# The down projection of a gated MLP as seven block products with sums formed in place, in place of twenty-two chunk steps

## The chip, the cores and the metric

The kernel runs on one core of one Trainium2 chip. The metric is the device time of one execution in microseconds (us); the time of a kernel is the median of its runs. Five engines work side by side: TensorE (PE) multiplies matrices, VectorE (DVE) and ScalarE (ACT) work on elements, GpSimd (POOL) is hardly used here, and SyncE (SP) issues the transfers. Each engine takes its instructions in one fixed order, and a wait at one instruction holds up all that stand behind it on that engine. All transfers of the part that is looked at here are issued on SP.

## The reference

The reference is one layer of a decoder trunk on 1024 tokens of width 1024 (`D`): four mixers, a gated merge, an output projection and a gated MLP. Only the end of the MLP is touched:

```python
D_FF = 256 * ((8 * D_MODEL // 3 + 255) // 256)      # 2816
# h = h + RMSNorm(GatedMLP(RMSNorm(h))), with a causal depthwise conv before the activation
def _rmsnorm(x, g):
    xf = x.astype(F32)
    y = xf * lax.rsqrt(jnp.mean(xf * xf, axis=-1, keepdims=True) + RMS_EPS)
    return (y * g.astype(F32)).astype(x.dtype)
```

The down projection multiplies the activated features, 1024 x 2816, by `f_down`, 2816 x 1024. Its result is normalised over the 1024 outputs of a token, scaled by a vector, and added to the residual h.

## The kernel before

**Three passes.** Every large float32 product is made of three passes in the format fp32r. A tile is split by `B.split`: ACT copies it into a high part (helper line L230), and DVE subtracts that from the tile to get the low part (L1190). `B.mm` then issues high by high, high by low and low by high into one PSUM bank (all matmuls are recorded at helper line L233). A tile that both engines have split is called cut below.

**Order.** The instructions of each engine are put in order when the kernel is built, by the scheduler of the tile framework, which simulates a timeline; pools and their buffer counts decide which tiles wait for which.

**The up projection** runs over 22 chunks of 128 features (`NFF`). It is already computed with seven block products in place of eight. For each chunk and each half of the tokens DVE and ACT make conv, activation and product, and the result `cg` (128 features x 512 tokens, last operation at L1645) is stored to the DRAM buffer `ad` (L1646). Feature chunk f of the activations is `ad[f]`, 128 x 1024 tokens.

**The down projection before** (L1670 to L1740) takes the outputs in two halves of 4 tiles of 128. *Half 0* runs over the 22 chunks: it loads 128 x 512 of `f_down` (tile `d`, L1682) and 128 x 1024 of `ad` (tile `w`, L1199), cuts both, and issues 24 matmuls of 512 columns for 4 output tiles and 2 token halves; all 8 PSUM banks collect sums over the 22 chunks. *Half 1* does the other 4 output tiles in three token blocks of 512, 256 and 256; the cut weights `drh`, `drl` are kept from the first block. After a block, `drain` copies the banks out (ACT), squares them (ACT) and adds the squares (DVE, L1703); `finish` sums the squares over the outputs with matmuls by ones, takes the inverse root (ACT Ln and Exp, each behind a load of its table, and four short DVE operations, L277 to L280, on the tile `nt`), spreads it with transposes (`ident`, L239), multiplies (L1708), adds the residual `hr` (L1709) and stores (L1710). `finish` of a block is placed inside the next block's matmuls.

Of the kernel before, what the change touches and what calls it, by code (L numbers as in the profile page):

```python
# [1225 lines left out]
def build(tc, I, out):  # L1226
# [443 lines left out]
    dp = ctx.enter_context(k.pool("dw", 2, side="right"))  # L1670
    hp = ctx.enter_context(k.pool("hres"))
    acp = ctx.enter_context(k.pool("acc"))
    wr = ctx.enter_context(k.pool("dres", side="right"))
    acc = [acp.tile([128, SEQ], F32, name=f"acc{n}") for n in range(KD)]
    HF = SEQ // 2
# [1 line left out]
    wres = {}

    def down_w(f, half):
        B.n += 1  # L1680
        r = dp.tile([128, 512], F32, tag="d0", name=f"d0_{half}{f}", bufs=3)
        nc.sync.dma_start(r[:], I["f_down"][128 * f:128 * f + 128, 512 * half:512 * half + 512])  # L1682
        if half:
            h, l = (wr.tile([128, 512], F32R, name=f"dr{q}{f}") for q in "hl")
        else:
            h, l = (dp.tile([128, 512], F32R, tag=f"d{q}", name=f"d{q}{f}") for q in "hl")
        B.split(r[:], h[:], l[:])
        return wtiles((h, l), 4)

    def drain(n, a, b, p, i):  # L1690

        L = b - a
        k.act(acc[n][:, a:b], p, AF.Copy)
        for c in ([(a, b)] if a < HF else [(HF, HF + TB), (HF + TB, SEQ)] if L > TB else [(a, b)]):
            key = (c, n % 2)
            m = c[1] - c[0]
            if n < 2:
                ss[key] = hp.tile([128, m], F32, name=f"fs{c[0]}_{n}")
                k.act(ss[key][:], acc[n][:, c[0]:c[1]], AF.Square)
            else:  # L1700
                sq = hp.tile([128, HF], F32, tag="fq", name=f"fq{c[0]}_{n}", bufs=2)
                k.act(sq[:, :m], acc[n][:, c[0]:c[1]], AF.Square)
                TT(ss[key][:], ss[key][:], sq[:, :m], ALU.add)  # L1703

    def finish(a, b, h):
        rs = rms_of(k, [ss[(a, b), 0][:], ss[(a, b), 1][:]], b - a)
        for n in range(KD):
            STT(acc[n][:, a:b], acc[n][:, a:b], k.V("n3", n), rs, ALU.mult, ALU.mult)  # L1708
            TT(h[:, n], h[:, n], acc[n][:, a:b], ALU.add)  # L1709
            nc.sync.dma_start(out[128 * n:128 * n + 128, a:b], h[:, n])  # L1710
# [47 lines left out]
```

## Time and profile before

| | us |
|---|---|
| median of 3 runs (1912.21 to 1915.57) | 1914.32 |
| the profiled execution, its own time | 1908.61 |
| its span from the first instruction to the last | 1906.8 |
| mean granted clock of TensorE in it, share of full speed | 0.983 |
| last matmul of the up projection starts | 1638.95 |
| last matmul of the down projection ends | 1890.9 |

The durations below are those of the profiled execution, whose own time lies 5.7 us under the median; 1.8 us of it lie outside the span. The down projection is the last stage: from the end of the up projection's matmuls to the end of its own it takes 251.7 us, and what follows (the last block's normalisation and stores) 15.9 us.

### The profile page before, as it was taken

How to read it: one execution, taken by the hardware profiler on the slowest of the kernel's cores; microseconds unless marked ns; L12 is line 12 of the kernel's file. 1: busy time of each engine (PE TensorE's matmuls, PEld its weight loads, DVE VectorE, ACT ScalarE, POOL GpSimd, SP SyncE). 2: the span in 40 equal slices, each digit the busy share in tenths (PEclk: the TensorE clock that was granted, in tenths of full speed). 3: DMA queues.
4: the chain of work that ended last, by engine and by line, in shares of the span. 5: the costliest groups of instructions: out<-in, count | busy, mean ns of one | idle time of the engine just before them, and what ended most of it. 6: DMA issues, size and time to landing. Idle time of an engine off the chain costs nothing.

```text
span 1906.8 us, 33092 instructions
## 1 busy us (share of the span) xinstructions
PE 1825.1 (96%) x13476; PEld 1714.7 (90%) x13476; DVE 1240.8 (65%) x2454; ACT 783.9 (41%) x1176; POOL 58.4 (3%) x87
## 2 busy tenths in 40 slices
PE   8999999999999998999999997799999999999997
PEld 7899999888888898989999897699999999888896
DVE  6566477562464557686368558899899998534444
ACT  4532121121361326363246476545444544324433
POOL 0000000000000000000025000000000000000000
PEclk9999999999999998999999899899999999999998
DMA  5024574574542143232676412223222222545433
GB/s 178 35 80 145 167 240 146 164 210 129 182 150 92 61 135 113 79 112 68 210 231 201 146 43 69 83 67 95 75 93 87 80 90 81 191 139 181 151 126 106
DMA packets 138761, 239.69 MB, mean 126 GB/s; under 512 B 22280, under 2 KB 82224, under 8 KB 137968
## 3 DMA queue, kind: packets, MB, share of 16 engines
q1 hardware_dynamic: 138608, 237.57, 39.1%
q8 instruction: 106, 1.74, 0.4%
q14 instruction: 47, 0.39, 0.1%
HBM read 166.02 MB, written 71.51 MB: 125 GB/s over the span
## 4 chain that ended last, share of the span: by engine, by line
PE 81%; DVE 7%; ACT 5%; DMA 3%; issue 2%; POOL 1%; SPq 0%; DVEq 0%; ACTq 0%; POOLq 0%
PE pm L233 47%; PE px L233 20%; PE py L233 13%; ACT L230 2%; ACT h_e L230 1%; POOL mg L1416 1%; PE px L239 1%; DMA s_ub<-s_su 0%; PE py L239 0%; DMA sb_h<-gd 0%; DVE acc L1708 0%; DVE ml L1190 0%; DMA h_rq<-p_h 0%; DMA p_h<-stg_h 0%; DMA p_m<-stg_m 0%
## 5 line engine op out<-in xcount | busy, mean ns | idle before, releaser
L233 PE MATMUL pm<-uh,w 128*128 128x342 f32 (+2 forms) x2688 | 660.6, 326 | 23.2 <-ACT w L230 8.3
L233 PEld LDWEIGHTS pm<-uh,w 128*128 128x128 f32 x2688 | 470.9, 190 | 33.5 <-ACT w L230 8.5
L233 PE MATMUL pm<-ul,w 128*128 128x342 f32 (+2 forms) x1344 | 439.9, 327 | 1.4 <-DVE ul L1260 1.4
L233 PEld LDWEIGHTS pm<-ul,w 128*128 128x128 f32 x1344 | 255.4, 190 | 8.6 <-issue 2.6
L230 ACT ACTIVATE w<-w 128x1024 fp32r<-128x1024 f32 (+2 forms) x111 | 116.3, 1048 | 290.1 <-PE pm L233 210.6
L1190 DVE TENSOR_TENSOR w<-w,w 128x1024 fp32r<-128x1024 f32 (+2 forms) x111 | 134.7, 1214 | 78.7 <-ACT w L230 77.4
L230 ACT ACT_TABLE_LOAD x78 | 100.1, 1283 | 8.0 <-DMA r_cb<-r_db 2.5
L233 PE MATMUL pm<-mh,woh 128*128 128x256 f32 (+1 forms) x192 | 55.5, 289 | 2.0 <-ACT woh L230 1.8
L233 PE MATMUL px<-w,drh 128*128 128x256 f32 (+1 forms) x220 | 57.2, 326 | 0.0
L233 PE MATMUL pm<-ml,woh 128*128 128x256 f32 (+1 forms) x192 | 55.5, 289 | 0.0
L233 PE MATMUL pm<-mh,wol 128*128 128x256 f32 (+1 forms) x192 | 54.8, 286 | 0.0
L1190 DVE TENSOR_TENSOR dl<-d,dh 128x512 fp32r<-128x512 f32 x22 | 15.2, 693 | 59.1 <-ACT dh L230 59.1
L233 PE MATMUL px<-w,dh 128*128 128x512 f32 x132 | 51.4, 396 | 0.0
L233 PE MATMUL pm<-w,dh 128*128 128x512 f32 x132 | 51.3, 396 | 0.0
L230 ACT ACTIVATE cg<-zg,fvec 128x512 f32<-128x512 f32 x44 | 35.6, 809 | 20.1 <-DVE zg L1638 20.0
L233 PE MATMUL pm<-w,drh 128*128 128x256 f32 (+1 forms) x176 | 42.2, 310 | 0.8 <-DVE w L1190 0.8
L230 ACT ACTIVATE dh<-d 128x512 fp32r<-128x512 f32 x22 | 13.9, 632 | 70.4 <-PE pm L233 70.2
L230 ACT ACTIVATE cg<-cg 128x512 f32<-128x512 f32 x44 | 27.7, 631 | 35.8 <-DVE cg L1643 35.6
L233 PEld LDWEIGHTS px<-w,drh 128*128 128x128 f32 x220 | 37.1, 188 | 4.1
L233 PEld LDWEIGHTS pm<-mh,woh 128*128 128x128 f32 x192 | 37.4, 195 | 2.5 <-ACT woh L230 2.5
L230 ACT ACTIVATE r_y<-px 128x128 f32<-128x128 f32 x17 | 4.7, 275 | 80.4 <-PE px L233 80.3
L233 PEld LDWEIGHTS pm<-ml,woh 128*128 128x128 f32 x192 | 37.4, 195 | 0.0
(780 smaller groups left out, 4923.1 us busy)
## 6 DMA issues: line engine op xcount, KB each, us to landing
fw<-in_f_up SPq DMA_DIRECT2D x46, 512.0 KB
w<-ad SPq DMA_DIRECT2D x43, 512.0 KB
w<-in_w_gate SPq DMA_DIRECT2D x32, 512.0 KB
w<-in_w_in SPq DMA_DIRECT2D x24, 512.0 KB
ad<-cg SPq DMA_DIRECT2D x44, 256.0 KB
d<-in_f_down SPq DMA_DIRECT2D x44, 256.0 KB
r_dw<-r_w SPq DMA_DIRECT2D x17, 256.0 KB
r_db<-r_tb SPq DMA_DIRECT2D x17, 256.0 KB
```

Of the source, the lines that this page charges most:

```text
L230: return self.nc.scalar.activation(out, in_, f, **kw)
L233: return self.nc.tensor.matmul(out, lhsT, rhs, start=start, stop=stop)
L239: return self.nc.tensor.matmul(out, in_, self.id[:], start=True, stop=True, is_transpose=True)
L1190: self.k.nc.vector.tensor_tensor(lo, src, hi, ALU.subtract)
L1416: (TT if n % 4 == 3 else G.tensor_tensor)(M[n], M[n], s[:], ALU.add)
```

## The change

The changed stage views the product as 2 x 2 blocks: the 22 feature chunks in two halves of 11 (`KH`), the outputs in two halves, the tokens in two halves. One level of Strassen's method, in Winograd's form, gives the four result blocks from seven block products. With `a` for weights (first index: output half; second: feature half, except that `a12` is feature half 1 of output half 0) and `b` for activations (feature half, token half), they are, in order:

P1 = a11·b11, P2 = a12·b21, P3 = s·t with s = a21+a22 and t = b12−b11, P4 = s·t with s ← s−a11 and t ← b22−t, P5 = a11·b11 with a11 ← a22−s and b11 ← t−b11, P6 = a22·(b21−t), P7 = (a12−s)·b22.

The results are c11 = P1+P2, U = P1+P4, c12 = U+P3+P7, and with U ← U+P5: c22 = U+P3 (in the tile `d_v`), c21 = U+P6 (in `d_u`). Each sum is written over a quarter that is no longer needed: `s`, `t`, `a11` and `b11` are changed in place between the products (L1699, L1775).

Each product runs over six groups of two chunks (the last has one). A group cuts its left operand (tiles `w1`, `w2`) and its right operand (tiles `bh`, `bl`), two buffers each, and issues 24 matmuls of 512 columns (12 in the last group). Four PSUM banks hold one product's result, so two products alternate. P7 is taken in two token blocks of 256, called P7a and P7b here; its cut operands are kept for the second. The tile tag `rw` has two buffers and serves two things: the loads of `a12` for P2 and for P7 (`rw_...`), and the scratch for squares (`sq_...`, L1750), which L1752 adds up. All of a12 and of b21 and b22 is loaded twice.

```diff
...
-    P = {(n, h): k.ps() for h in range(2) for n in range(4)}
-    for f in range(NFF):
-        w = down_w(f, 0)
-        A = B.weights(ad[f], SEQ)
-        for h in range(2):
-            for n in range(4):
-                B.mm(P[n, h][:], w[n:n + 1], [(A[0][:, HF * h:HF * h + HF], A[1][:, HF * h:HF * h + HF])], first=f == 0, last=f == NFF - 1)
-    for h in range(2):
-        for n in range(4):
-            drain(n, HF * h, HF * h + HF, P[n, h][:], n)
-    todo = None
-    for a, b in ((0, HF), (HF, HF + TB), (HF + TB, SEQ)):
-        L = b - a
-        hr = hp.tile([128, KD, L], F32, tag=f"h{L}", name=f"hr{a}")
-        nc.sync.dma_start(hr[:], hd[:, :, a:b].rearrange("q p t -> p q t"))
-        P = [k.ps() for _ in range(4)]
-        m = D // L
-        for f in range(NFF):
-            if not a:
-                wres[f] = down_w(f, 1)
-            if f % m == 0:
-                q = min(m, NFF - f)
-                A = wtiles(B.weights(ad[f:f + q, :, a:b].rearrange("f p t -> p f t"), q * L), q, L)
-            for n in range(4):
-                B.mm(P[n][:, :L], wres[f][n:n + 1], [A[f % m]], first=f == 0, last=f == NFF - 1)
-            if todo and f == 3:
-                finish(*todo)
-        for n in range(4):
-            drain(4 + n, a, b, P[n][:, :L], n)
-        todo = (a, b, hr)
-    finish(*todo)
+    KH, HF = NFF // 2, SEQ // 2
+    groups = [(f, min(2, KH - f)) for f in range(0, KH, 2)]
+    def kept(tag, g, dt=F32):
+        k.n += 1
+        return dn.tile([128, groups[g][1], 512], dt, tag=f"{tag}{g}", name=f"{tag}{g}_{k.n}")[:]
+    def brief(tag, g):
+        k.n += 1
+        p = dn if tag == "rw" else B.wp
+        return p.tile([128, D], F32, tag=tag, name=f"{tag}_{k.n}", **({"bufs": 2} if tag == "rw" else {}))[:, :512 * groups[g][1]].rearrange("p (q c) -> p q c", c=512)
+    def left(t, n, h, g):
+        f, w = groups[g]
+        f += KH * h
+        nc.sync.dma_start(t, I["f_down"][128 * f:128 * (f + w), 512 * n:512 * n + 512].rearrange("(q p) c -> p q c", p=128))
+        return t
+    def right(t, h, s, g):
+        f, w = groups[g]
+        f += KH * h
+        nc.sync.dma_start(t, ad[f:f + w, :, HF * s:HF * s + HF].rearrange("f p t -> p f t"))
+        return t
+    def sub(o, x, y):
+        TT(o, x, y, ALU.subtract)
+        return o
+    def cut(src, g, tags=None):
+        w = groups[g][1]
+        k.n += 1
+        if isinstance(tags, tuple):
+            h, l = (kept(t, g, F32R) for t in tags)
+        elif tags:
+            h, l = (B.wp.tile([128, D], F32R, tag=t, name=f"{t}_{k.n}")[:, :512 * w].rearrange("p (q c) -> p q c", c=512) for t in ("w1", "w2"))
+        else:
+            h, l = (dn.tile([128, 2, 512], F32R, tag=t, name=f"{t}_{k.n}", bufs=2)[:, :w] for t in ("bh", "bl"))
+        B.split(src, h, l)
+        return h, l
+    def terms(P, g, L, R, a=0, b=512):
+        f, w = groups[g]
+        for i in range(w):
+            for n in range(4):
+                B.mm(P[n][:, :b - a], [tuple(t[:, i, 128 * n:128 * n + 128] for t in L)], [tuple(t[:, i, a:b] for t in R)],
+                     first=f + i == 0, last=f + i == KH - 1)
+    def product(l, r):
+        P = [k.ps() for _ in range(4)]
+        for g in range(len(groups)):
+            L, R = cut(l(g), g, True), cut(r(g), g)
+            terms(P, g, L, R)
+        return P
+    big = lambda name: dn.tile([128, 4, 512], F32, name=name)
+    q = {t: {} for t in ("a11", "a22", "s", "b11", "t")}
+    def have(t, v, *at):
+        return lambda g: q[t].setdefault(g, v(kept(t, g), *at, g))
+    a11, a22, a21 = have("a11", left, 0, 0), have("a22", left, 1, 1), have("s", left, 1, 0)
+    b11, b12 = have("b11", right, 0, 0), have("t", right, 0, 1)
+    a12 = lambda g: left(brief("rw", g), 0, 1, g)
+    b21, b22 = (lambda s: lambda g: right(brief("w0", g), 1, s, g))(0), (lambda s: lambda g: right(brief("w0", g), 1, s, g))(1)
+    U, V5, c11, c12 = (big(f"d_{t}") for t in ("u", "v", "c11", "c12"))
+    ss = {}
+    def squares(key, C, a, b):
+        for i in (0, 2):
+            if key not in ss:
+                ss[key] = dn.tile([128, 2, b - a], F32, name=f"ss{key}")
+                k.act(ss[key][:], C[:, 0:2, a:b], AF.Square)
+                continue
+            k.n += 1
+            t = dn.tile([128, D], F32, tag="rw", name=f"sq_{k.n}", bufs=2)[:, :2 * (b - a)].rearrange("p (q c) -> p q c", q=2)
+            k.act(t, C[:, i:i + 2, a:b], AF.Square)
+            TT(ss[key][:], ss[key][:], t, ALU.add)
+    def scaled(C, m, a, b):
+        for n in range(4):
+            k.act(C[:, n, a:b], C[:, n, a:b], AF.Copy, scale=k.V("n3", m + n))
+    def finish(key, parts, o, a, b):
+        rs = rms_of(k, [ss[key][:, i] for i in range(2)], b - a)
+        for C, m in parts:
+            for i in (0, 2):
+                k.n += 1
+                h = dn.tile([128, 2, 512], F32, tag="bh" if i else "bl", name=f"hr_{k.n}", bufs=2)[:, :, :b - a]
+                nc.sync.dma_start(h, hd[m + i:m + i + 2, :, o + a:o + b].rearrange("q p t -> p q t"))
+                c = C[:, i:i + 2, a:b]
+                TT(c, c, b3(rs, 2), ALU.mult)
+                TT(h, h, c, ALU.add)
+                nc.sync.dma_start(out[128 * (m + i):128 * (m + i) + 256, o + a:o + b].rearrange("(q p) t -> p q t", p=128), h)
+    for n, p in enumerate(product(a11, b11)):
+        k.act(U[:, n], p[:], AF.Copy)
+    for n, p in enumerate(product(a12, b21)):
+        TT(c11[:, n], U[:, n], p[:], ALU.add)
+    P = product(lambda g: (lambda x, y: (TT(x, x, y, ALU.add), x)[1])(a21(g), a22(g)), lambda g: sub(b12(g), q["t"][g], q["b11"][g]))
+    for n, p in enumerate(P):
+        k.act(V5[:, n], p[:], AF.Copy)
+    squares(0, c11, 0, HF)
+    scaled(c11, 0, 0, HF)
+    P = product(lambda g: sub(q["s"][g], q["s"][g], q["a11"][g]), lambda g: sub(q["t"][g], b22(g), q["t"][g]))
+    for n, p in enumerate(P):
+        TT(U[:, n], U[:, n], p[:], ALU.add)
+    for i in (0, 2):
+        TT(c12[:, i:i + 2], U[:, i:i + 2], V5[:, i:i + 2], ALU.add)
+    P = product(lambda g: sub(q["a11"][g], q["a22"][g], q["s"][g]), lambda g: sub(q["b11"][g], q["t"][g], q["b11"][g]))
+    for n, p in enumerate(P):
+        TT(U[:, n], U[:, n], p[:], ALU.add)
+    for i in (0, 2):
+        TT(V5[:, i:i + 2], U[:, i:i + 2], V5[:, i:i + 2], ALU.add)
+    def b4(g):
+        x = b21(g)
+        return sub(x, x, q["t"][g])
+    P = product(lambda g: q["a22"][g], b4)
+    last = (0, TB), (TB, HF)
+    for a, b in last:
+        squares(1 + a, V5, a, b)
+    scaled(V5, 4, 0, HF)
+    for n, p in enumerate(P):
+        TT(U[:, n], U[:, n], p[:], ALU.add)
+    squares(0, U, 0, HF)
+    scaled(U, 4, 0, HF)
+    LR = {}
+    todo = 0, ((c11, 0), (U, 4)), 0, 0, HF
+    for a, b in last:
+        P = [k.ps() for _ in range(4)]
+        for g in range(len(groups)):
+            if not a:
+                x = a12(g)
+                LR[g] = cut(sub(x, x, q["s"][g]), g, ("a11", "a22")), cut(b22(g), g, ("b11", "t"))
+            terms(P, g, *LR[g], a, b)
+            if g == 1:
+                finish(*todo)
+        for n, p in enumerate(P):
+            TT(c12[:, n, a:b], c12[:, n, a:b], p[:, :b - a], ALU.add)
+        squares(1 + a, c12, a, b)
+        scaled(c12, 0, a, b)
+        todo = 1 + a, ((V5, 4), (c12, 0)), HF, a, b
+    finish(*todo)
     ctx.close()
```

**SP where the stage begins.** The rows are transfers in the order of SP; `ad<-cg` are the up projection's stores, `d_0...` and `w_9...` the loads of `f_down` and `ad` before. Before:

```order
L1646 DMA ad<-cg_1_16731 128x512
L1646 DMA ad<-cg_0_16913 128x512
L1682 DMA d_00_17408<-in_f_down 128x512
L1682 DMA d_01_17444<-in_f_down 128x512
L1682 DMA d_02_17480<-in_f_down 128x512
L1682 DMA d_03_17516<-in_f_down 128x512
L1682 DMA d_04_17552<-in_f_down 128x512
L1646 DMA ad<-cg_0_17029 128x512
L1199 DMA w_95_17486<-ad 128x1024
L1646 DMA ad<-cg_1_17145 128x512
L1199 DMA w_97_17522<-ad 128x1024
L1646 DMA ad<-cg_1_17261 128x512
```

After; `a_9...` and `b_9...` are the left and right operands of P1's groups:

```order
L1646 DMA ad<-cg_1_16731 128x512
L1646 DMA ad<-cg_0_16913 128x512
L1646 DMA ad<-cg_0_17029 128x512
L1646 DMA ad<-cg_1_17145 128x512
L1646 DMA ad<-cg_1_17261 128x512
L1688 DMA a_965_17391<-in_f_down 128x2x512
L1695 DMA b_967_17397<-ad 128x2x512
L1688 DMA a_969_17427<-in_f_down 128x2x512
L1695 DMA b_971_17433<-ad 128x2x512
```

Before, two `ad` loads and five `f_down` loads stand ahead of the last three stores; now every load of P1 stands behind the last store of `cg`.

**DVE from P2 into P3.** Before, DVE does in this stage one low part of each kind for each chunk:

```order
L1190 TENSOR_TENSOR dl_17519<-d_03_17516,dh_17518 128x512
L1190 TENSOR_TENSOR w_97_17524<-w_97_17522,w_97_17523 128x1024
L1190 TENSOR_TENSOR dl_17555<-d_04_17552,dh_17554 128x512
L1190 TENSOR_TENSOR w_99_17560<-w_99_17558,w_99_17559 128x1024
L1190 TENSOR_TENSOR dl_17591<-d_05_17588,dh_17590 128x512
L1190 TENSOR_TENSOR w_101_17596<-w_101_17594,w_101_17595 128x1024
```

After, from P2's last adds on (`d_c` is c11, `d_u` is U, `w_...` and `bl_...` at L1190 are the low parts for P3's groups, `s`, `t`, `a_9...` and `b_9...` at L1699 the sums for P4 and P5):

```order
L1774 TENSOR_TENSOR d_c_17385<-d_u,pm_17599 128x512
L1774 TENSOR_TENSOR d_c_17385<-d_u,px_17600 128x512
L1190 TENSOR_TENSOR bl_17828<-t_1024_17824,bh_17827 128x1024
L1774 TENSOR_TENSOR d_c_17385<-d_u,py_17601 128x512
L1699 TENSOR_TENSOR s_1021_17815<-s_1021_17815,a_965_17391 128x1024
L1774 TENSOR_TENSOR d_c_17385<-d_u,pm_17602 128x512
L1190 TENSOR_TENSOR w_1028_17861<-s_1026_17855,w_1028_17860 128x1024
L1190 TENSOR_TENSOR bl_17868<-t_1029_17864,bh_17867 128x1024
L1699 TENSOR_TENSOR t_1024_17824<-w_1057_18065,t_1024_17824 128x1024
L1699 TENSOR_TENSOR a_965_17391<-a_1022_17817,s_1021_17815 128x1024
L1752 TENSOR_TENSOR ss_18047<-ss_18047,sq_18049 128x1024
L1699 TENSOR_TENSOR s_1026_17855<-s_1026_17855,a_969_17427 128x1024
```

The piece goes on in this way: between P2's first add and the second low part of P4's first group (`bl_18069`), both included, stand 42 rows on DVE, 32 of 128x1024 and 10 of 128x512. All sums of P4 and of P5 are among them.

**DVE and ACT in P7a.** Before, the four short operations for the first block's inverse root stand side by side on DVE:

```order
L1190 TENSOR_TENSOR w_169_18883<-w_169_18881,w_169_18882 128x1024
L277 TENSOR_SCALAR nt_18791<-px_18782 128x4
L278 SCALAR_TENSOR_TENSOR nt_18791<-nt_18791 128x4
L279 TENSOR_TENSOR nt_18791<-nt_18791 128x4
L280 SCALAR_TENSOR_TENSOR nt_18791<-nt_18791 128x4
L1708 SCALAR_TENSOR_TENSOR acc_17392<-acc_17392,vecs,pm_18798 128x512
```

After, `rw_...` at L1699 is a12−s of a group, `a_11...` at L1190 its low part, and `nt_18789` the inverse root of the first token half:

```order
L1699 TENSOR_TENSOR rw_18706<-rw_18706,s_1021_17815 128x1024
L1699 TENSOR_TENSOR rw_18743<-rw_18743,s_1026_17855 128x1024
L1190 TENSOR_TENSOR a_1123_18710<-rw_18706,a_1122_18709 128x1024
L1190 TENSOR_TENSOR t_1173_18942<-w_1170_18939,b_1172_18941 128x512
L1190 TENSOR_TENSOR a_1131_18747<-rw_18743,a_1130_18746 128x1024
L1699 TENSOR_TENSOR rw_18821<-rw_18821,s_1031_17895 128x1024
L1699 TENSOR_TENSOR rw_18858<-rw_18858,s_1036_17935 128x1024
L1190 TENSOR_TENSOR a_1145_18825<-rw_18821,a_1144_18824 128x1024
L277 TENSOR_SCALAR nt_18789<-pm_18780 128x4
L1190 TENSOR_TENSOR a_1153_18862<-rw_18858,a_1152_18861 128x1024
L278 SCALAR_TENSOR_TENSOR nt_18789<-nt_18789 128x4
L279 TENSOR_TENSOR nt_18789<-nt_18789 128x4
```

On ACT the same stretch reads (`a_11...<-rw_...` is a high part of a12−s; the two rows on `nt` are Ln and Exp):

```order
L230 ACTIVATE a_1122_18709<-rw_18706 128x1024
L230 ACTIVATE b_1172_18941<-w_1170_18939 128x512
L230 ACTIVATE a_1130_18746<-rw_18743 128x1024
L230 ACTIVATE a_1144_18824<-rw_18821 128x1024
L230 ACT_TABLE_LOAD
L230 ACTIVATE nt_18789<-pm_18780,epsv 128x4
L230 ACT_TABLE_LOAD
L230 ACTIVATE nt_18789<-nt_18789 128x4
L230 ACTIVATE a_1152_18861<-rw_18858 128x1024
```

The short operations are now apart: between the first and the second stands the low part `a_1153_18862`, whose high part stands on ACT behind the Exp. In PE's order the transposes of this inverse root stand between P7a's second and third group.

## Rows read from the trace of the kernel before

**Rows 1.** The page, busy time of each engine over the span.

```profile
PE 1825.1 (96%) x13476; PEld 1714.7 (90%) x13476; DVE 1240.8 (65%) x2454; ACT 783.9 (41%) x1176; POOL 58.4 (3%) x87
```

**Rows 2.** Windows: stretch, length, busy time of each engine, granted clock, DMA share, GB/s.

```profile
1639.20:1762.50 123.30, 123.30 (x529) 99.08 (x528) 49.41 (x56) 41.86 (x57) 0.00 (x0) 1.00 0.53 173
1639.20:1890.90 251.70, 250.90 (x1351) 214.16 (x1349) 107.83 (x145) 91.54 (x135) 0.00 (x0) 1.00 0.48 155
1890.90:1906.80 15.90, 1.78 (x11) 1.25 (x10) 8.21 (x24) 4.65 (x10) 0.00 (x0) 0.63 0.20 66
```

**Rows 3.** Groups of instructions by line and shape, window from 1500.

```profile
L1190 DVE TENSOR_TENSOR w<-w,w 128x1024 fp32r<-128x1024 f32 x43 | 52.7, 1225 | 48.1 <-ACT w L230 48.1
...
L230 ACT ACTIVATE w<-w 128x1024 fp32r<-128x1024 f32 x43 | 45.4, 1055 | 54.9 <-PE py L233 24.7 <-PE pm L233 16.8 <-PE px L233 10.4
...
L1190 DVE TENSOR_TENSOR dl<-d,dh 128x512 fp32r<-128x512 f32 x22 | 15.2, 693 | 59.1 <-ACT dh L230 59.1
...
L230 ACT ACTIVATE dh<-d 128x512 fp32r<-128x512 f32 x22 | 13.9, 632 | 70.4 <-PE pm L233 70.2 <-DMA d<-in_f_down 0.2
```

**Rows 4.** Waits, window from 1500: sum, times, longest, in us.

```profile
ACT dh L230 <- PE pm L233: 70.2, 20, 4.0
...
DVE w L1190 <- ACT w L230: 53.5, 41, 5.4
```

**Rows 5.** Timeline of DVE: start, length, line, operation, count.

```profile
1190.92 2.35 DVE L1488 TENSOR_TENSOR z<-z,x 128x1024 f32<-128x1024 f32 x2
...
1837.21 5.36 DVE L1708 SCALAR_TENSOR_TENSOR acc<-acc,vecs,pm 128x512 f32<-128x512 f32 x8 [1.82 <-PE pm L239]
...
1844.82 3.69 DVE L1709 TENSOR_TENSOR hr<-hr,acc 128x512 f32<-128x512 f32 x6
```

**Rows 6.** Timeline where the up projection ends: SP, PE and DVE.

```profile
1635.71 0.32 SPq L1199 DMA_DIRECT2D w<-ad  x1
...
1638.95 0.29 PE L233 MATMUL pm<-t4h,a22l 128*128 128x258 f32 x1
...
1639.08 0.63 PE L233 MATMUL px<-w,dh 128*128 128x512 f32 x2
...
1642.71 0.69 DVE L1645 TENSOR_TENSOR cg<-cg,cv 128x512 f32<-128x512 f32 x1
...
1643.43 0.32 SPq L1646 DMA_DIRECT2D ad<-cg  x1
```

**Rows 7.** Windows around two stretches of loads (columns of group 2).

```profile
1638.00:1638.50 0.50, 0.50 (x7) 0.50 (x6) 0.28 (x1) 0.18 (x1) 0.00 (x0) 1.00 0.82 328
1638.50:1639.00 0.50, 0.50 (x7) 0.50 (x6) 0.00 (x0) 0.50 (x1) 0.00 (x0) 1.00 0.17 66
1648.00:1649.00 1.00, 1.00 (x6) 0.82 (x5) 0.00 (x0) 0.00 (x0) 0.00 (x0) 1.00 1.04 387
1653.00:1654.00 1.00, 1.00 (x6) 0.79 (x5) 0.10 (x1) 0.00 (x0) 0.00 (x0) 1.00 1.10 352
1658.00:1660.00 2.00, 2.00 (x10) 1.63 (x9) 0.00 (x0) 0.51 (x1) 0.00 (x0) 1.00 1.03 408
```

**Rows 8.** Windows around an idle stretch of PE (columns of group 2).

```profile
1188.00:1189.00 1.00, 0.00 (x0) 0.00 (x0) 1.00 (x2) 0.00 (x0) 0.00 (x0) 1.00 0.00 0
1206.00:1207.00 1.00, 0.00 (x0) 0.00 (x0) 0.26 (x1) 0.98 (x2) 0.00 (x0) 0.50 0.00 0
1214.00:1215.00 1.00, 1.00 (x7) 1.00 (x6) 1.00 (x2) 1.00 (x2) 0.00 (x0) 0.50 0.00 0
1216.00:1217.00 1.00, 1.00 (x11) 1.00 (x10) 1.00 (x2) 0.23 (x1) 0.00 (x0) 1.00 0.00 0
```

**Rows 9.** Timeline of PE and ACT: work after that idle stretch; the first block's normalisation.

```profile
1212.64 0.58 PE L233 MATMUL pm<-b22h,s4h 128*128 128x258 f32 x1 [3.60 <-ACT b22h L230]
...
1831.13 1.84 PE L233 MATMUL px<-ones,fs 128*128 128x1 f32 x16
...
1836.57 0.60 PE L239 MATMUL pm<-ident,nt 128*128 128x128 f32 x4
...
1831.24 1.28 ACT L230 ACT_TABLE_LOAD   x1
```

More of the change, by code (lines that the diff above doesn't have):

```diff
@@ L1668, in build @@
     cua.close()
[L1670 to L1675, printed above, removed]
-    ss = {}
[L1677 to L1688, printed above, removed]
@@ L1690, in drain @@
-    def drain(n, a, b, p, i):
-        L = b - a
[L1693 to L1710, printed above, removed]
-    P = {(n, h): k.ps() for h in range(2) for n in range(4)}
-    for f in range(NFF):
-        w = down_w(f, 0)
-        A = B.weights(ad[f], SEQ)
-        for h in range(2):
-            for n in range(4):
-                B.mm(P[n, h][:], w[n:n + 1], [(A[0][:, HF * h:HF * h + HF], A[1][:, HF * h:HF * h + HF])], first=f == 0, last=f == NFF - 1)
@@ L1719, in build @@
-    for h in range(2):
-        for n in range(4):
-            drain(n, HF * h, HF * h + HF, P[n, h][:], n)
-    todo = None
-    for a, b in ((0, HF), (HF, HF + TB), (HF + TB, SEQ)):
-        L = b - a
-        hr = hp.tile([128, KD, L], F32, tag=f"h{L}", name=f"hr{a}")
-        nc.sync.dma_start(hr[:], hd[:, :, a:b].rearrange("q p t -> p q t"))
+    dn = ctx.enter_context(k.pool("down", side="right"))
+    KH, HF = NFF // 2, SEQ // 2
+    groups = [(f, min(2, KH - f)) for f in range(0, KH, 2)]
```

## Prediction

> **What bounds the kernel now.** I read the busy times first: PE is busy for 96% of the span and DVE for 65% [rows 1]. That is a mean over unlike stages, so the stage that changes was read next, by windows. From 1639.2 to 1890.9 us PE is busy for 250.9 of 251.7 us, DVE for 107.8 and ACT for 91.5, at a granted clock of 1.00; behind it follow 15.9 us of normalisation and stores [rows 2]. Then the waits: ACT waits for PE to give back buffers of the cut tiles (70.2 us at the `dh` copies), and DVE for ACT behind that [rows 4]. So PE sets this stage, everything else runs ahead of it, and 528 matmuls of 512 columns take 123.3 us [rows 2], 0.2335 us each. Half 0 and half 1 hold 1056 such, 246.6 us; the other 5.1 us are the two inner normalisations and small gaps.
>
> The sum below is for this stage, in the profiled execution (own time 1908.6). Its median over the runs shown is 1914.3, 5.7 us more; I add the difference of the stage to the median.
>
> **1. What is removed: matmuls.** Seven products of 11 chunks, 4 output tiles and 3 passes are 924 matmuls of 512 columns (P7 in halves of 256 at half the price): 924 x 0.2335 = 215.8 us. Against 251.7 that is 35.9 us less, if PE never waits. All that follows asks where it will.
>
> **2. The start.** Before, the first down matmul stands at 1639.08, 0.13 us behind the last up matmul at 1638.95 [rows 6], because its loads had been issued ahead of the last stores. Now SP has every load of P1 behind the last `ad<-cg` store. That store is issued at 1643.43, after the last L1645 on DVE (1642.71 + 0.69) [rows 6]; this does not move. An issue takes 0.32 us, so `a_965` goes out at about 1643.8 and `b_967` just behind. One 512 KB load alone was issued at 1635.71 [rows 6], and its bytes stop between 1638.5 and 1639.0 [rows 7], about 2.9 us; the second adds 0.52 MB at about 390 GB/s (1.3 us). Landed at 1648.0, and the high part on ACT 1.055 us [rows 3]: first matmul at 1649.1. **PE idles 9.9 us** (5 if the loads land at once, 12 if each takes its 2.9 alone).
>
> **3. The clock.** After an idle stretch the granted clock was 0.50 (its 1.2 GHz level) both in the idle and at work, with 7 matmuls a us at 1214 and 11 at 1216, where it is 1.00 (2.4 GHz) again; work had begun at 1212.64 [rows 8, 9]. In an idle stretch before, at 1188, it had stayed 1.00 [rows 8]. So a restart costs 3.4 us at 7/11 to 1/2 of the rate, 1.2 to 1.7 us; I take **1.5 us** here.
>
> **4. The loads of P1 and P2.** By the order on SP, 16.5 MB go out up to the operands of P2's third group (P1's 5.8, two groups of a12, all of P3's three quarters, 8.6, and the third group itself). PE needs them at 1649.1 + 1.5 + 30.9 (P1) + 11.2 (two groups) = 1692.7. While transfers are queued the rows show 387, 352 and 408 GB/s [rows 7], mean 382: 43.2 us, landed at 1687.1, with the high part 1688.2. **No stall**; the cover is 4.5 us, gone below some 350 GB/s.
>
> **5. DVE's load in P3.** From P2's first addition to the low part that P4's first group needs, DVE has 42 rows in one piece, with all sums of P4 and P5 among them. Nothing in the trace has this form with both inputs in place, so I bound it: two 1024-wide additions took 2.35 us together [rows 5], a low part alone 1.225 [rows 3], six 512-wide additions 3.69 and eight 5.36 [rows 5]. Run back to back, 1.15 for 1024 and 0.63 for 512: 32 x 1.15 + 10 x 0.63 = 43.1 us. DVE can begin 1.2 us before P2's end, since the first bank is complete six matmuls early. PE has P3 (30.9 us) and P4's four high by high matmuls (0.9) to do meanwhile. 43.1 − 1.2 − 30.9 − 0.9 = **10.1 us lost**, spread over P3's later groups and P4's first. Bounds: 5 (1.0 us an operation), 14 (1.225 and 0.693, no overlap). This is a stage in which DVE, idle for more than half of it before, sets the time.
>
> **6. Starts of P5 and P6.** Two of the four additions into U stand before the right operand's low part. The second ends with P4's last matmul, the low part 1.15 us later; four matmuls cover 0.9. With the semaphores some **1.0 us each, 2.0** (0 to 3).
>
> **7. P7.** Times from P6's end. The left operand a12−s needs a12 again, in a `rw` buffer that the squares' scratch holds until L1752 has read it. DVE comes to that row after the four additions into U and another low part: first addition from −1.2, then 4 x 0.63 + 1.15 + 1.15, ends at 3.6; load issued at 4.0, landed 6.9. The two sums L1699 on DVE (1.15 for the first), then ACT's copy (1.05) behind the copies and scalings of its queue: about 1.2 more for that queue and semaphores. First matmul at **10.5**, where before the next block's matmuls followed at once. Two groups (5.6) and the ones matmuls (1.7 between their start and the next row; the row shows 1.84) [rows 9] bring PE to 17.8. There the transposes wait for `nt`. Third group's a12 can load only when the first low part is done (11.5): landed 14.4, sum 15.6, high part 16.7; then a table load of 1.28 [rows 9], Ln, another, Exp: 19.9; the fourth group's high part 21.0, its low part 22.2 on DVE ahead of the other three short operations: 22.9. PE idles from 17.8 to **23.0**. With transposes (0.6) [rows 9], 1.15 for the smaller normalisation in P7b and 30.9 of matmuls P7 takes 50.1 us, **19.2 over its matmuls**. A clock drop in the first wait is absorbed in the second; one behind the second costs **1.5**. Before, the same chain ran from 1831.13 to the transposes at 1836.57 with PE at work [rows 9]; were it covered so here, P7 would stand at 14.0 and no second restart.
>
> **8. The end** stays the 15.9 us [rows 2]: the last block is again 256 tokens, with the same chain.
>
> **Sum:** 215.8 + 9.9 + 1.5 + 10.1 + 2.0 + 19.2 + 1.5 = 260.0 us in place of 251.7, **+8.3 us**: 1916.9 by the profiled execution, **1922.6 by the median (+0.4%)**.
>
> **The rivals.**
>
> *Transfers slower.* The loads of 2 KB rows run among stores and at 330 GB/s or less; 352 is in the rows [rows 7]. At 330 the 16.5 MB end at 1694 and P2 stalls 3.8 us (1926); at 250, 20 us (1942). For it: twice loaded quarters in one queue. Against: 387 and 408.
>
> *DVE keeps up.* If the 42 rows take 33 us or less, the 10.1 us vanish: 1912.5, within the bound of no change. It needs 0.88 us for 1024, where every row has 1.15 or more; or PE's groups finding their low parts early enough, which only shifts the backlog to P4.
>
> *P7 without its waits* (the faster side). If a12's loads got a free buffer before the squares take it, P7 would cost its matmuls and 3.5 us: 17.2 less, 1905.4. It decides from 12.1 us less on, that is if P7's two waits and the restart, 17.2 us here, come to 5.1 or less. Against: the pool has two buffers, both hold squares there, and the additions into U stand ahead of L1752 on DVE.
>
> *Cutting the busiest engine pays in full.* With PE at 250.9 of 251.7 us [rows 2] the stage would shrink by the 132 matmuls taken out, 30.8 us, and the waits above would be lost in buffers that run ahead, as ACT and DVE do now [rows 4]: 1883.5. The Trainium skill, Perfetto Trace Analysis, section "Identifying the Most-Contended Engine", says this: find the engine with the highest occupancy and optimize it first, and for TensorE go by the weight load's busy share, here 90%. The trace agrees on which engine that is; it does not show that the others can follow at the new pace, and at P3 their rows say they can't.
>
> **How the numbers follow.** A measurement tells about 0.2%, 3.8 us, from no change. Forecast 0.52, its own range 1916 to 1930 (start 5 to 12, P3 5 to 14, P7 14 to 22); slower transfers 0.16; DVE keeps up 0.14; P7 without waits 0.11; paid in full 0.07. Slower: 0.50 of the forecast and 0.16, 0.66. Same: 0.14 and 0.02 of the forecast, 0.16. Faster: 0.18. The range 1904 to 1936 leaves out the paid-in-full case, near half of the case without P7's waits and a quarter of the slow transfers, under 0.2.
>
> **What the profile after would show.** First P1 matmul some 10 us behind the last up matmul, released by ACT's high part, its load issued right behind the last store; granted clock 0.50 then 1.00. P1 and P2 without gaps (a gap released by DMA in P2 speaks for slow transfers). In P3 DVE busy for nearly all of it, PE waiting on L1190 in its later groups and at P4's start, some 10 us in all. At P7 a PE gap of 10 us with an a12 load behind L1752, and one of 5 us at the transposes. I am wrong above all if DVE's in-place sums overlap better than back to back rows say, if PE's two waits in P7 shrink below half, or if SP's queue holds P2 back.

## The result and the profile after

| | before | after |
|---|---|---|
| median of 4 runs each, us | 1914.11 (1912.21 to 1915.57) | 1932.61 (1930.10 to 1933.21) |
| ratio after to before, 95% interval | | 1.0095 (1.0077 to 1.0112) |
| the profiled execution: own time, span | 1908.61, 1906.8 | 1932.13, 1930.4 |
| last up matmul ends (its start and 0.25) | 1639.2 | 1645.1 |
| from there to the last down matmul's end | 251.7 | 268.4 |
| from there to the end of the span | 15.9 | 16.9 |

The kernel became slower by 0.95%, some 18 us; +8.3 us had been forecast (1922.6). The two spans differ by 23.6 us, but 5.9 of that had arisen before the changed stage, where the order of TensorE's instructions is the same in both. In the profiles of the eight further kernels below that point lies anywhere from 1641.8 to 1654.9 us, and the profiled execution of before is 5.5 us under its median where that of after lies at its own. So I put it down to the execution and not to the change, and all comparisons below are of the time from the last up matmul to the end of the span: 267.6 us before, **285.3 after, +17.7**, which agrees with the medians.

The page's busy times, which answer to [rows 1]:

```profile
PE 1813.2 (94%) x13212; PEld 1699.2 (88%) x13212; DVE 1314.0 (68%) x2492; ACT 797.7 (41%) x1167; POOL 58.4 (3%) x87
```

PE has less work and a smaller share of the span, DVE more of both. The windows answer to [rows 2], [rows 7] and [rows 8] (columns as there):

```profile
1670.00:1680.00 10.00, 10.00 (x44) 8.07 (x43) 7.38 (x7) 3.53 (x4) 0.00 (x0) 1.00 1.05 386
1736.00:1738.00 2.00, 2.00 (x6) 1.54 (x5) 2.00 (x3) 0.00 (x0) 0.00 (x0) 0.50 0.00 0
1764.00:1766.00 2.00, 2.00 (x6) 1.52 (x6) 2.00 (x3) 0.00 (x0) 0.00 (x0) 0.50 0.00 0
1870.00:1880.00 10.00, 8.15 (x38) 8.15 (x39) 6.95 (x7) 3.58 (x4) 0.00 (x0) 0.50 0.34 107
...
1645.10:1913.50 268.40, 232.06 (x1087) 191.60 (x1086) 182.07 (x193) 107.08 (x128) 0.00 (x0) 0.93 0.39 136
```

Over the stage PE is busy for 232.1 of 268.4 us, where before it was 250.9 of 251.7. The second, third and fourth rows are at the 0.50 clock, inside the stage: before, the stage was at 1.00 throughout. While P1 runs the queue moves 386 GB/s. What PE waited for in the stage, up to 1913.5 us (us in total, times, longest):

```profile
PE px L233 <- ACT a L230: 14.4, 1, 14.4
PE px L233 <- ACT bh L230: 11.3, 1, 11.3
PE px L233 <- DVE bl L1190: 5.5, 4, 2.2
PE pm L233 <- DVE bl L1190: 3.7, 2, 2.9
PE px L239 <- DVE nt L280: 1.5, 1, 1.5
```

The start of the stage, to be read against [rows 6]; PE, DVE, SP and ACT in turn:

```profile
1644.82 0.28 PE L233 MATMUL pm<-t4h,a22l 128*128 128x258 f32 x1
1656.40 0.80 PE L233 MATMUL px<-bh,w 128*128 128x512 f32 x1 [11.30 <-ACT bh L230]
...
1648.57 0.69 DVE L1645 TENSOR_TENSOR cg<-cg,cv 128x512 f32<-128x512 f32 x1
...
1649.70 0.38 SPq L1688 DMA_DIRECT2D a<-in_f_down  x1
1650.18 0.46 SPq L1695 DMA_DIRECT2D b<-ad  x1
...
1653.88 1.06 ACT L230 ACTIVATE w<-a 128x1024 fp32r<-128x1024 f32 x1 [6.21 <-DMA a<-in_f_down]
1655.29 1.06 ACT L230 ACTIVATE bh<-b 128x1024 fp32r<-128x1024 f32 x1 [0.35 <-DMA b<-ad]
```

The last store waits for L1645 on DVE (1648.57 + 0.69), P1's first two loads are issued at 1649.70 and 1650.18, and ACT has them at 1653.88 and 1655.29: 4.2 and 5.1 us from their own issue. From the first issue to the second landing it is 5.6 us, where 4.2 (2.9 and 1.3) had been taken. PE idles for 11.3 us. Next, every wait of PE from P3's start to P7a's transposes:

```profile
1721.82 0.50 PE L233 MATMUL px<-bl,w 128*128 128x512 f32 x1 [0.78 <-DVE bl L1190]
...
1735.50 0.78 PE L233 MATMUL px<-bl,w 128*128 128x512 f32 x1 [2.22 <-DVE bl L1190]
...
1750.27 0.49 PE L233 MATMUL px<-bl,w 128*128 128x512 f32 x1 [1.73 <-DVE bl L1190]
...
1761.82 0.50 PE L233 MATMUL pm<-bl,w 128*128 128x512 f32 x1 [2.90 <-DVE bl L1190]
...
1795.21 0.50 PE L233 MATMUL px<-bl,w 128*128 128x512 f32 x1 [0.78 <-DVE bl L1190]
...
1827.05 0.50 PE L233 MATMUL pm<-bl,w 128*128 128x512 f32 x1 [0.77 <-DVE bl L1190]
...
1871.85 0.58 PE L233 MATMUL px<-b,a 128*128 128x256 f32 x1 [14.38 <-ACT a L230]
...
1885.82 0.65 PE L239 MATMUL px<-ident,nt 128*128 128x128 f32 x4 [1.45 <-DVE nt L280]
```

A wait of this kind comes behind the four high by high matmuls of a group (0.93 us) and so also dates the product: P3 begins at 1721.82 − 0.78 − 0.93 = 1720.1, P4 at 1758.0, P5 at 1793.5, P6 at 1825.35, and P6 ends at 1871.85 − 14.38 = 1857.5. P1 and P2 took 63.7 us, P3 37.9, P4 35.5, P5 31.8, P6 32.1, P7 56.0, each of 30.9 us of matmuls. What stood ahead of P7's first matmul, on SP, ACT and DVE:

```profile
1857.27 1.14 SPq L1765 DMA_DIRECT2D hr<-hd  x2
1859.41 0.36 SPq L1695 DMA_DIRECT2D w<-ad  x1
1861.74 0.37 SPq L1688 DMA_DIRECT2D rw<-in_f_down  x1
...
1867.25 1.06 ACT L230 ACTIVATE b<-w 128x1024 fp32r<-128x1024 f32 x1 [1.75 <-DMA w<-ad]
...
1868.34 1.23 DVE L1190 TENSOR_TENSOR t<-w,b 128x1024 fp32r<-128x1024 f32 x1 [2.80 <-ACT b L230]
1869.48 2.36 DVE L1699 TENSOR_TENSOR rw<-rw,s 128x1024 f32<-128x1024 f32 x2
```

The a12 load (`rw`) went out at 1861.74, 4.3 us behind P6's end, as forecast. But the b22 load of 1859.41 stands behind the residual's loads (`hr`), lands only at 1867.25, and its low part (1868.34) stands ahead of a12−s (1869.48) on DVE.

### The profile page after: what moved, and what is told of

The parts are those of the page before. It is cut to its first block, busy times and chain, and to the rows that moved or that the text cites. A ratio compares the mean times of both kernels' runs of the same rounds, so it can differ in the third digit from the quotient of the medians.

```text
span 1930.4 us, 32490 instructions
## 1 busy us (share of the span) xinstructions
PE 1813.2 (94%) x13212; PEld 1699.2 (88%) x13212; DVE 1314.0 (68%) x2492; ACT 797.7 (41%) x1167; POOL 58.4 (3%) x87
## 4 chain that ended last, share of the span: by engine, by line
PE 77%; DVE 10%; ACT 5%; DMA 4%; issue 3%; POOL 1%; SPq 0%; DVEq 0%; ACTq 0%; POOLq 0%
PE pm L233 46%; PE px L233 18%; PE py L233 12%; ACT L230 2%; DVE w L1190 1%; DMA w<-ad 1%; ACT h_e L230 1%; PE px L239 1%; POOL mg L1416 1%; ACT w L230 0%; DMA s_ett<-s_det 0%; PE py L239 0%; DVE ml L1190 0%; DMA h_rq<-p_h 0%; DVE bl L1190 0%
## 5 line engine op out<-in xcount | busy, mean ns | idle before, releaser
L230 ACT ACTIVATE w<-w 128x1024 fp32r<-128x1024 f32 (+1 forms) x66 | 69.8, 1057 | 224.7 <-PE pm L233 195.8
L1190 DVE TENSOR_TENSOR w<-w,w 128x1024 fp32r<-128x1024 f32 (+1 forms) x66 | 80.7, 1223 | 26.9 <-ACT w L230 25.6
L233 PE MATMUL px<-bh,w 128*128 128x512 f32 x198 | 79.9, 403 | 11.3 <-ACT bh L230 11.3
L233 PE MATMUL pm<-bh,w 128*128 128x512 f32 x198 | 74.8, 402 | 0.0
L233 PEld LDWEIGHTS px<-bh,w 128*128 128x128 f32 x198 | 38.3, 193 | 20.7 <-ACT bh L230 11.5
L233 PE MATMUL py<-bh,w 128*128 128x512 f32 x132 | 52.8, 400 | 0.0
L233 PEld LDWEIGHTS pm<-bh,w 128*128 128x128 f32 x198 | 38.0, 192 | 9.0
L233 PE MATMUL px<-bl,w 128*128 128x512 f32 x99 | 40.5, 409 | 5.5 <-DVE bl L1190 5.5
L1190 DVE TENSOR_TENSOR w<-a,w 128x1024 fp32r<-128x1024 f32 (+1 forms) x18 | 20.4, 1136 | 36.6 <-ACT w L230 36.5
L233 PE MATMUL pm<-bl,w 128*128 128x512 f32 x99 | 40.4, 408 | 3.7 <-DVE bl L1190 3.7
```

Source lines behind the costliest of these rows:

```text
L230: return self.nc.scalar.activation(out, in_, f, **kw)
L233: return self.nc.tensor.matmul(out, lhsT, rhs, start=start, stop=stop)
L1190: self.k.nc.vector.tensor_tensor(lo, src, hi, ALU.subtract)
```

## The experiments

Ratios are to the kernel before, run beside them; "stage and tail" is the time from the last up matmul to the end of the span in the profile (267.6 before, 285.3 after). Each of these is read from one profiled execution. Where the kernels share a wait it repeats to 0.5 us (11.3 to 11.7 us ahead of P1, 13.9 to 14.4 ahead of P7), but the granted clock doesn't repeat so well (experiment 4), so that a difference under some 4 us in stage and tail is not certain by itself; single waits are compared below.

**1. The squares' scratch apart from a12's buffers.**

```diff
-            t = dn.tile([128, D], F32, tag="rw", name=f"sq_{k.n}", bufs=2)...
+            t = dn.tile([128, D], F32, tag="sq", name=f"sq_{k.n}", bufs=1)...
```

> The squares' scratch gets a tag of its own (one buffer), so that the loads of a12 for P7 no longer wait for it. In the changed kernel PE idled 14.4 us ahead of P7, and P7 took 57.0 us from P6's end to its last matmul, where its matmuls are 30.9. Theory A (the scratch holds up a12 and with it all of P7's start): the first wait goes below 1 us and P7 takes 36 to 40 us; time 1913 to 1917. Theory B (the wait is that of the right operand b22, whose loads stand behind 2.1 MB of residual on SP): the wait only moves to P7's third or fourth group, 5 to 10 us there, and the time is 1920 to 1926.

Measured: 1.0033 (1.0005 to 1.0062), stage and tail 272.4 us, 12.9 less. PE's timeline, P6 and P7:

```profile
1841.47 0.50 PE L233 MATMUL pm<-bl,w 128*128 128x512 f32 x1 [2.68 <-DVE bl L1190]
...
1860.46 0.28 PE L233 MATMUL px<-b,a 128*128 128x256 f32 x1
```

P7 follows P6 without a wait (1860.46) and takes 35.8 us in place of 56.0 (which the expectation gave as 57.0): theory A, and no jam at the later groups. The time fell by less than that, and not into the 1913 to 1917 us expected (median 1917.92). a12−s and its low parts now stand in P6, where PE waits 2.7 us (1841.47) and P6 takes 35.0; P3 and P4 are 1.5 us longer, and the last block's end 2.6 us.

**2. The first residual left out.** The output lacks the residual of the first token half; its loads on SP become zeros by GpSimd.

```diff
-                nc.sync.dma_start(h, hd[...])
+                if key:
+                    nc.sync.dma_start(h, hd[...])
+                else:
+                    nc.gpsimd.memset(h, 0.0)
```

> The first token half's residual is left out (its four loads of 512 KB, ahead of the last b22 loads on SP, become zeros written by GpSimd), all else as in the changed kernel. Theory A (the scratch): the wait ahead of P7 stays at 14 us, the a12 loads being issued 4.3 us after P6's end as now; time within 2 us of 1932.6. Theory B (the queue behind the residual): the b22 loads land some 5 us earlier, the two low parts ahead of a12-s on DVE go with them, the wait falls to 10 to 11 us, as the prediction had it, and the time to about 1928.5.

Measured: 1.0066 (1.0044 to 1.0088), stage and tail 281.4 us, 3.9 less. P7's first matmul:

```profile
1872.15 0.58 PE L233 MATMUL px<-b,a 128*128 128x256 f32 x1 [11.02 <-ACT a L230]
```

The wait is 11.0 us in place of 14.4. So both causes are real and lie one behind the other: the scratch gives the 10.5 to 11 us of the forecast, and the 2.1 MB of residual in the queue ahead of b22 the 3.4 us that it missed. With a12 free (experiment 1) the second costs nothing: there DVE makes a12−s already in P6, ahead of b22's low parts.

**3. P5's sums left out.** P5 is made from a11 and b11 as loaded, so the output is another; DVE has twelve operations less ahead of P4's first low part.

```diff
-    P = product(lambda g: sub(q["a11"][g], q["a22"][g], q["s"][g]), lambda g: sub(q["b11"][g], q["t"][g], q["b11"][g]))
+    P = product(lambda g: q["a11"][g], lambda g: q["b11"][g])
```

> P5 takes a11 and b11 as they are: its twelve sums are left out, 12.5 us of DVE work that stood inside P3. In the changed kernel P3 took 37.9 us and P4 35.5, where each has 30.9 of matmuls; DVE was busy without a break over P3. Theory DVE (PE waits for low parts behind the sums, and twice the granted clock falls behind that wait): DVE's piece ends 1 us before PE's need, the waits on L1190 in P3 and at P4's start fall from 7.6 to below 1.5 us, no 0.50 clock in P3 and P4, both take 31 to 32 us, time 1920 to 1922. Rival (the waits come from the order of ACT's copies or from PSUM banks): P3 and P4 stay above 35 us, time above 1929.

Measured: 1.0053 (1.0027 to 1.0079), stage and tail 277.5 us, 7.8 less. The waits of PE at the starts of P3, P4 and P5, the only ones there:

```profile
1732.81 0.50 PE L233 MATMUL px<-bl,w 128*128 128x512 f32 x1 [0.78 <-DVE bl L1190]
...
1764.81 0.50 PE L233 MATMUL pm<-bl,w 128*128 128x512 f32 x1 [0.72 <-DVE bl L1190]
...
1796.65 0.50 PE L233 MATMUL px<-bl,w 128*128 128x512 f32 x1 [0.77 <-DVE bl L1190]
```

P3 takes 32.1 us and P4 31.8, 9.5 less together, and no stretch at 0.50 is left in them. The stalls are DVE's sums.

**4. P1's first group loaded early**, from buffers that are free during the up projection; a11 and b11 of that group are loaded a second time, behind P1.

```diff
-    for n, p in enumerate(product(a11, b11)):
+    for n, p in enumerate(product(lambda g: a11(g) if g else left(brief("w0", g), 0, 0, g), lambda g: b11(g) if g else right(brief("w0", g), 0, 0, g))):
         k.act(U[:, n], p[:], AF.Copy)
+    a11(0), b11(0)
```

> P1's first group takes its two operands from the two buffers of tag w0, which are free before the up projection ends; their loads then stand ahead of the last five stores on SP. a11 and b11 of that group are loaded once more for later use. Theory (the start's 11.3 us are the loads behind the last store): the first matmul comes 3.7 us after the last up matmul, ruled by ACT's high part behind the last activation, then 0.8 us for the low part and about 1 us at the second group, whose loads still stand behind the store; stage start 5.5 us in place of 11.3, a clock restart perhaps gone; time 1925 to 1927. Rival (the same wait moves whole to the second group, whose loads land at the old time): 1930 to 1932.

Measured: 1.0081 (1.0057 to 1.0105), stage and tail 283.5 us, only 1.8 less. P1's first matmul, and two new waits in P2:

```profile
1648.02 0.79 PE L233 MATMUL px<-bh,w 128*128 128x512 f32 x1 [3.67 <-ACT bh L230]
...
1684.61 0.50 PE L233 MATMUL pm<-bl,w 128*128 128x512 f32 x1 [1.94 <-DVE bl L1190]
...
1699.09 0.80 PE L233 MATMUL pm<-bh,w 128*128 128x512 f32 x1 [3.95 <-ACT bh L230]
```

The start falls from 11.3 to 3.7 us as expected, and there is no wait in P1. What I had not expected is that P2 waits 5.9 us: its operands come too late. The forecast had given their cover as 4.5 us; 7.6 us of earlier start and 1 MB more to load use it up. With the clock at 0.50 behind the start and behind the second of these waits, P1 and P2 take 73.3 us in place of 63.7, and P3 begins 77.0 us behind the last up matmul, where it was 75.0 after the change. So the early start alone gained nothing up to there. The 1.8 us come from P3 and P4, which take 3.7 us less together with the same instructions: PE waits 2.21 us (up to 1736.70) and 2.68 us (up to 1760.68) at the same two places as after the change, but the clock stays at 1.00 behind them. The windows (columns as in [rows 2]):

```profile
1699.00:1704.00 5.00, 4.91 (x12) 3.85 (x13) 3.69 (x4) 2.15 (x3) 0.00 (x0) 0.50 0.62 206
1737.00:1739.00 2.00, 2.00 (x10) 1.60 (x9) 2.00 (x3) 0.00 (x0) 0.00 (x0) 1.00 0.00 0
```

The ratio can't be told from the changed kernel's 1.0095 either.

**5. P2's operands ahead of P3's.** With experiment 4's start, P2's blocks are loaded into the results' tiles, which are still free, so that SP issues them ahead of P3's 8.7 MB; the second load of a11 and b11 moves behind P2.

```diff
+    lent = {2: V5[:, 0:2], 3: V5[:, 2:4], 4: c12[:, 0:2], 5: c12[:, 2:3]}
+    lend = {2: c11[:, 0:2], 3: c11[:, 2:4], 4: dn.tile(...)..., 5: c12[:, 3:4]}
-    for n, p in enumerate(product(a12, b21)):
+    for n, p in enumerate(product(lambda g: left(lent[g], 0, 1, g) if g in lent else a12(g), lambda g: right(lend[g], 1, 0, g) if g in lend else b21(g))):
...
+    a11(0), b11(0)
```

> P1's first group early as before (the first matmul 3.7 us after the last up matmul), and P2's operands into tiles that are still free (the results' tiles), so that their loads stand ahead of P3's 8.7 MB on SP; the second load of a11 and b11 stands behind them. With the early start alone PE then waited 1.9 and 4.0 us in P2, and most of the gain was given back. Theory (those waits are P2's operands behind P3's in the queue): no wait in P1 or P2 over 1.2 us, stage and tail 276 to 278 us (283.5 with the early start alone). Rival (the queue's total rate is the limit): the waits stay within 1.5 us of 5.9 in P1, P2 and the start of P3 together, 282 to 284 us.

Measured: stage and tail 278.4 us, 6.9 less than after the change and 5.1 less than with the early start alone; ratio 1.0075 (1.0048 to 1.0102), which by itself can't be told from 1.0081. All waits of PE up to P3:

```profile
1651.63 0.80 PE L233 MATMUL px<-bh,w 128*128 128x512 f32 x1 [3.67 <-ACT bh L230]
...
1659.71 0.49 PE L233 MATMUL px<-bh,w 128*128 128x512 f32 x1 [0.71 <-ACT bh L230]
...
1718.01 0.51 PE L233 MATMUL px<-bl,w 128*128 128x512 f32 x1 [0.77 <-DVE bl L1190]
```

The waits in P2 are gone, and P1 and P2 take 64.7 us in place of 73.3: it was the place in the queue and not its rate. Of the 6.9 us some 1.6 are again P3 and P4.

**6. P5's sums on GpSimd**, in place, all else as in the changed kernel.

```diff
+    def psub(o, x, y):
+        nc.gpsimd.tensor_tensor(o, x, y, ALU.subtract)
+        return o
-    P = product(lambda g: sub(q["a11"][g], q["a22"][g], q["s"][g]), lambda g: sub(q["b11"][g], q["t"][g], q["b11"][g]))
+    P = product(lambda g: psub(q["a11"][g], q["a22"][g], q["s"][g]), lambda g: psub(q["b11"][g], q["t"][g], q["b11"][g]))
```

> P5's twelve sums are made by GpSimd, in place, where it was idle; all else as in the changed kernel. One such sum takes GpSimd 2.3 to 2.5 us by the additions of the merge, 26 us in all, and P5 needs them only after P4. Theory DVE (the sums' place on DVE is what stalls P3 and P4): as with the sums left out, waits on L1190 of about 1.5 us in P3 and P4 together, each product 31 to 32 us, the stage and tail 277 to 278 us in place of 285.3, time 0.4% under the changed kernel. Rival (GpSimd and DVE slow each other when both read the same tiles): DVE's 1024-wide operations take over 1.3 us, P3 and P4 stay above 66 us together.

Measured: 1.0168 (1.0134 to 1.0202), stage and tail 300.2 us, 14.9 **more**. GpSimd and DVE in P3:

```profile
1731.19 3.20 POOL L1787 TENSOR_TENSOR a<-a,s 128x1024 f32<-128x1024 f32 x1 [1.22 <-DVE s L1699]
1734.35 3.32 POOL L1787 TENSOR_TENSOR b<-t,b 128x1024 f32<-128x1024 f32 x1
...
1732.11 3.35 DVE L1190 TENSOR_TENSOR w<-s,w 128x1024 fp32r<-128x1024 f32 x1
1735.39 3.36 DVE L1190 TENSOR_TENSOR bl<-t,bh 128x1024 fp32r<-128x1024 f32 x1
1738.67 1.21 DVE L1699 TENSOR_TENSOR s<-s,a 128x1024 f32<-128x1024 f32 x1
```

DVE's 1024-wide operation takes 1.21 us where GpSimd is idle and 3.35 us where it works: the two of 1732.11 and 1735.39 end 1.1 us behind GpSimd's of 1731.19 and 1734.35, about their own length, as if they had begun behind them. The Trainium skill, SBUF — State Buffer, section "SBUF: two separate sides", says that a DVE operation with two inputs in SBUF and a GpSimd operation that reads SBUF lock each other out for a whole instruction. The trace agrees: 1.21 against 3.35. PE's waits at P3's third group and at P4's first:

```profile
1738.80 0.80 PE L233 MATMUL px<-bl,w 128*128 128x512 f32 x1 [7.43 <-DVE bl L1190]
...
1772.44 0.79 PE L233 MATMUL pm<-bl,w 128*128 128x512 f32 x1 [4.85 <-DVE bl L1190]
```

P3 and P4 take 87.5 us together in place of 73.4. The rival held; theory DVE is not touched by it, since the sums still hold up DVE, from another engine.

**7. All of 1, 5 and 6, the finish a group later.**

```diff
-            if g == 1:
+            if g == 2:
                 finish(*todo)
```

> All corrections together: own scratch for the squares, P5's sums on GpSimd, P1's first group early, P2's operands ahead of P3's in the queue, and the first normalisation's finish a group later in P7. If the losses add up as they were measured one by one (12.9, 8 and 8 us), stage and tail take 256 to 258 us where the kernel before takes 267.6: 1903, ratio 0.994 to the kernel before. Rival (the reliefs overlap, DVE or the transfers being short again in P6 and P7): 262 to 268 us, a ratio of 0.997 to 1.000.

Measured: 1.0055 (1.0038 to 1.0071), stage and tail 278.5 us. The waits for DVE's low parts:

```profile
PE px L233 <- DVE bl L1190: 17.1, 5, 8.6
PE pm L233 <- DVE bl L1190: 7.2, 3, 3.7
```

24.3 us, against 9.2 after the change: most of what the rest gained, the sums on GpSimd lose. Neither range of the expectation holds.

**8. The same with P5's sums on DVE**, in tiles of two-buffered tags, which keeps the scheduler from placing them all in P3.

```diff
+    P = product(lambda g: sub(brief("rw", g), q["a22"][g], q["s"][g]), lambda g: sub(brief("w0", g), q["t"][g], q["b11"][g]))
```

> As the version with all corrections, but P5's sums go back to DVE, into two-buffered tiles of the tags rw and w0, so that at most two groups of them can be made ahead of P5's own cuts; four of the twelve are still placed in P3. Theory (DVE's pace and GpSimd's share of it decide): DVE's 1024-wide operations take 1.22 us again, its piece in P3 is 26 x 1.135 + 8 x 0.60 = 34.3 us and ends about 1 us behind PE's need, P3 and P4 take 64 to 68 us together; stage and tail 258 to 264 us where the kernel before has 267.6 and the changed kernel 285.3; ratio to the kernel before 0.995 to 0.998. Rival (P5 and P6, with eight sums and P7's operands, become DVE's next jam): waits of 4 us or more in P5 or P6, 266 to 272 us, no change against the kernel before.

Measured: **0.9952 (0.9935 to 0.9969)**, stage and tail 258.4 us. PE's largest waits:

```profile
PE pm L233 <- DVE bl L1190: 6.3, 3, 2.9
PE pm L233 <- DVE ss L1752: 4.1, 1, 4.1
PE px L233 <- ACT bh L230: 3.7, 1, 3.7
PE px L233 <- DVE bl L1190: 3.6, 4, 1.1
```

This version beats both kernels: 9.2 us under the kernel before in the stage and tail, 26.9 under the changed one. The single gains of experiments 1, 3 and 5 (12.9, 7.8, 6.9) would give 257.7. That this comes within 0.7 us is in part chance, since experiment 3 left out sums that are made here, and the later finish was not tried alone; in experiment 1, with the finish at its old place, PE waited only 0.4 us at the transposes of P7a.

## Why the prediction had the sign and half of the size

The direction, and that the seven products would lose in waits what they save in matmuls, were right, at each of the places named. The size was not: +8.3 forecast, +17.7 measured. Term by term, forecast to measured:

| term | forecast | measured |
|---|---|---|
| matmuls | 215.8 | 215.8 (seven times 30.9, by the pitch) |
| 2. the start | 9.9 | 11.3 |
| 3. the clock behind it (P1 and P2 over their 61.7) | 1.5 | 2.0 |
| 4. the loads of P2 | 0 | 0 |
| 5. DVE's load in P3, up to P4's first low part | 10.1 | 9.9 |
| the clock behind that wait, in P4 | not counted | 1.8 |
| 6. starts of P5 and P6 (over 30.9 each) | 2.0 | 2.2 |
| 7. P7 over its matmuls, with its restart | 20.7 | 25.1 |
| 8. the end | 15.9 | 16.9 |

**Step 7 failed by most**: its first wait took 14.4 us where the sum had 10.5 (its own terms add to 10.3). "Load issued at 4.0" held for a12 (issued at 4.3). What it left out is the right operand: the low parts of b22 stand ahead of a12−s on DVE, and the b22 load stands behind 2.1 MB of residual on SP. I had followed the queue of DVE up to L1752 only, and that of SP not at all for the rows ahead of mine. Experiment 2 prices it at 3.4 us of the 3.9. Step 7 also said that "a clock drop in the first wait is absorbed in the second". It was not quite: P7a's first groups ran at 0.50 for some 10 us (up to about 1882.3), where step 3's rows had 3.4, so that PE was ready for the transposes 12.5 us behind its first matmul in place of 7.3, waited 1.45 us there in place of 5.2, and began them at 14.0 in place of 12.5. The 1.5 us for a restart behind that wait did not come: the clock was 1.00 there. With the 3.9 this leaves 0.5 of the 4.4 us unexplained.

**Step 2** took 2.9 us for one load alone and 1.3 for the second as the price of two in a queue that fills behind them: 4.2 us, where 5.6 passed from the first issue to the second landing. This is the whole 1.4 us. That experiment 4 takes 7.6 us off the wait shows that it is these loads; that they share the rate with those behind them is not shown.

**Steps 3 and 5, the clock.** The sum had no term for the clock behind the waits of P3 and P4. The granted clock fell to 0.50 behind the waits of 2.2 and 2.9 us (1736 to 1738, 1764 to 1766), and not behind the one of 1.7 us. Within P3 this cost nothing that shows, since DVE worked on without a break; behind the last wait P4 took 1.8 us more. But the length of the wait alone does not decide it: in experiment 4 waits of 2.21 and 2.68 us at the same places left the clock at 1.00, in experiment 8 one of 2.92 us did, and in the kernel before an idle stretch of 3.3 us, around 1188, had done so [rows 8]:

```profile
1190.40 0.39 PE L233 MATMUL pm<-t2h,s2l 128*128 128x258 f32 x1 [3.33 <-DVE s2l L1190]
```

What decides it stays open here. The Trainium skill, TensorE: Matmul & The Clock Gate, section "Loop structure matters more than you think", tells of the drop at long DMA waits, with a copy by DVE as harmless where the matmuls follow at once; here it came behind short waits for DVE, in some executions.

**Step 8** took the end as before. It took 1.0 us more: PE waited 3.15 us for the last sums of squares on DVE (L1752), where it had waited 1.70 for those of L1703.

**Right:** step 5 to 0.2 us. The 42 operations took 42.4 us back to back (1719.35 to 1761.77), where 43.1 had been taken, and began 0.75 us ahead of P2's end, where 1.2 had been taken. The two errors cancel in part, but the mechanism is the one forecast, and experiment 3 shows that the sums are the cause. Right too were step 4, with a cover small enough to be used up in experiment 4, and step 6. Of the rivals, slow transfers did not come (386 GB/s), DVE did not keep up, P7 kept its waits, and cutting the busiest engine did not pay in full: after the change it is busy for 232 of 268 us.

That a version of the same products is 0.5% faster than the kernel before shows that the losses belong to the order and the buffers, and not to the seven products. What stays open: in experiment 8 the last block's end takes 19.6 us, 2.7 more than after the change. The trace shows DVE finishing the block before (L1767, L1768) between the last two sums of squares, and PE waiting 4.1 us for them in place of 3.1; no experiment changed that.

## What to carry to other kernels

Here fewer matmuls paid only once DVE, which makes the sums, kept up with PE's new pace in each product. So add up DVE's operations product by product, in the order in which they will stand, and see which are placed earlier than they are needed. Where one buffer or one queue serves two purposes, follow each operand of the first matmul behind it back through every queue, the transfers' too. And a start that is made earlier should be followed to the next load: here it was lost again 40 us later until the queue was put in order.
